# Giving each partition 128 KiB of neighbouring memory per turn, instead of two places 8 MiB apart

## The chip, the cores and the metric

The kernel runs on one core of a Trainium2 chip; the other cores are idle. The metric is the device time of that core in microseconds (us). Executions of one kernel agree within about 0.1%, unless said otherwise. A ratio is the mean time of one kernel's fast runs over that of the other's of the same rounds, so not quite the ratio of the medians quoted beside it.

## The reference

The backward pass of log-softmax over the last axis, in fp32:

```python
# y, dy: (8, 1024, 8192) fp32, so 8192 rows of 8192
softmax_x = np.exp(y)
sum_dy = np.sum(dy, axis=-1, keepdims=True)
return (dy - softmax_x * sum_dy).astype(np.float32)
```

Each element of y and dy is read once and each element of the result is written once: three tensors of 268.44 MB, 805.3 MB in all.

## The kernel before

The 8192 rows form 32 groups of 256; a partition holds two rows (64 KiB) of a group. A turn of the loop treats two groups. Three tiles of 64 KiB per partition exist: `x_ts[0]` and `x_ts[1]` for dy, overwritten by the result, and one `y_t`, which both groups of a turn share. The sums are split between VectorE (first row) and ScalarE (second row). Exp runs on ScalarE, multiply-add on VectorE, in pieces. All DMAs are issued by SyncE.

```python
y_v = y.flatten_outer_dims().rearrange("(g p r) d -> g p (r d)", p=P, r=R)      # R = 2
dy_v = dy.flatten_outer_dims().rearrange("(g p r) d -> g p (r d)", p=P, r=R)
out_v = out.flatten_outer_dims().rearrange("(g p r) d -> g p (r d)", p=P, r=R)
# ... (pools, tiles, sums() and compute() cut)
def load_dy(g, x):
    nc.sync.dma_start(out=x[:], in_=dy_v[g])
def load_y(g, lo, hi):
    nc.sync.dma_start(out=y_t[:, lo:hi], in_=y_v[g][:, lo:hi])
# ...
for g in range(0, G, 2):
    load_dy(g, x_ts[0])
    load_y(g, 0, W)
    s_t = sums(x_ts[0])
    for r in range(R):
        compute(x_ts[0], s_t, r)
    load_dy(g + 1, x_ts[1])
    s_t = sums(x_ts[1])
    for r in range(R):
        load_y(g + 1, r * D, (r + 1) * D)
        compute(x_ts[1], s_t, r)
    for j in range(2):
        nc.sync.dma_start(out=out_v[g + j], in_=x_ts[j][:])
```

## Time and profile before

| | before |
|---|---|
| time, median of the three runs known at the prediction | 1866.96 us (1866.71 to 1867.38) |
| span of the profiled run | 1865.9 us |
| VectorE / ScalarE busy | 46% / 37% |
| DMA queue: share of the 16 engines' time | 99.9% |
| rate over the span | 432 GB/s |

Read it from the bottom up. A queue that keeps 16 DMA engines busy for 99.9% of the span leaves nothing for anything else to bound, provided that the engines are not slow while busy.

### The profile page before, as it was taken

How to read it: one execution, taken by the hardware profiler on the slowest of the kernel's cores; microseconds unless marked ns; L12 is line 12 of the kernel's file. 1: busy time of each engine (PE TensorE's matmuls, PEld its weight loads, DVE VectorE, ACT ScalarE, POOL GpSimd, SP SyncE). 2: the span in 40 equal slices, each digit the busy share in tenths (PEclk: the TensorE clock that was granted, in tenths of full speed). 3: DMA queues.
4: the chain of work that ended last, by engine and by line, in shares of the span. 5: the costliest groups of instructions: out<-in, count | busy, mean ns of one | idle time of the engine just before them, and what ended most of it. 6: DMA issues, size and time to landing. Idle time of an engine off the chain costs nothing.

```text
span 1865.9 us, 923 instructions
## 1 busy us (share of the span) xinstructions
DVE 859.8 (46%) x256; ACT 698.7 (37%) x321; POOL 0.2 (0%) x4
## 2 busy tenths in 40 slices
DVE  2907429074290732807328073280632806338063
ACT  2606326063260532605336052360523605236052
POOL 0000000000000000000000000000000000000000
DMA  9999999999999999999999999999999999999999
GB/s 427 424 430 427 430 447 427 427 431 445 427 427 441 426 437 434 438 431 427 437 438 429 433 428 440 434 431 437 425 438 436 433 436 425 439 433 436 434 428 391
DMA packets 16135, 805.37 MB, mean 432 GB/s; under 512 B 1792, under 2 KB 1792, under 8 KB 1792
## 3 DMA queue, kind: packets, MB, share of 16 engines
q1 hardware_dynamic: 16128, 805.31, 99.9%
q14 instruction: 7, 0.06, 0.0%
HBM read 536.87 MB, written 268.44 MB: 432 GB/s over the span
## 4 chain that ended last, share of the span: by engine, by line
DMA 64%; DVE 13%; ACT 10%; another core or an unknown queue 9%; issue 1%; SPq 0%; DVEq 0%; ACTq 0%
DMA x<-in_dy_dram 31%; DMA out_dram<-x 30%; DVE x L81 13%; ACT copied L61 6%; ACT y_t L80 4%; DMA y_t<-in_y_dram 3%; SPq L75 0%; DVEq L128 0%; ACTq L128 0%; SPq L52 0%; ACTq L80 0%; ACTq L61 0%
## 5 line engine op out<-in xcount | busy, mean ns | idle before, releaser
L81 DVE SCALAR_TENSOR_TENSOR x<-y_t,s_t,x 128x3072 f32<-128x3072 f32 (+1 forms) x192 | 579.4, 3059 | 255.7 <-ACT y_t L80 255.7
L57 DVE TENSOR_REDUCE s_t<-x 128x1 f32<-128x8192 f32 x32 | 277.8, 8682 | 722.3 <-DMA x<-in_dy_dram 722.3
L80 ACT ACTIVATE y_t<-y_t 128x3072 f32<-128x3072 f32 (+1 forms) x192 | 460.1, 2466 | 269.4 <-DMA y_t<-in_y_dram 253.2
L61 ACT ACTIVATE copied<-x 128x4096 f32<-128x4096 f32 x64 | 229.6, 3587 | 864.9 <-DMA x<-in_dy_dram 863.9
L61 ACT ACTIVATION_READ_ACCUMULATOR copied<-x 128x1 f32 x64 | 11.9, 186 | 0.0
L64 DVE TENSOR_SCALAR s_t<-half_t 128x1 f32<-128x1 f32 x32 | 6.5, 204 | 0.0
L61 ACT ACT_TABLE_LOAD x1 | 1.3, 1283 | 0.7 <-PEq L117 0.7
L117 POOL MEMSET const-bfloat16-1.0<- 128x1 bf16 x1 | 0.1, 101 | 0.0
L117 POOL MEMSET const-uint8-127<- 128x1 uint8 x1 | 0.1, 101 | 0.0
L117 POOL MEMSET const-float32-0.0<- 128x1 f32 x1 | 0.1, 98 | 0.2 <-issue 0.2
L117 POOL MEMSET const-float32-1.0<- 128x1 f32 x1 | 0.1, 98 | 0.0
## 6 DMA issues: line engine op xcount, KB each, us to landing
y_t<-in_y_dram SPq DMA_DIRECT2D x32, 4096.0 KB, 18.1
x<-in_dy_dram SPq DMA_DIRECT2D x32, 48.3
out_dram<-x SPq DMA_DIRECT2D x32, 32.5
y_t<-in_y_dram SPq DMA_DIRECT2D x16, 57.6
```

Of the source, the lines that this page charges most:

```text
L57: nc.vector.tensor_reduce(out=s_t[:, 0:1], in_=x[:, :D], axis=mybir.AxisListType.X, op=ALU.add, negate=True)
L61: nc.scalar.activation(copied[:], x[:, D + h * H : D + (h + 1) * H], COPY, accum_out=half_t[:, h : h + 1])
L64: nc.vector.tensor_scalar(out=s_t[:, 1:2], in0=half_t[:, 0:1], scalar1=half_t[:, 1:2], scalar2=-1.0, op0=ALU.add, op1=ALU.mult,)
L80: nc.scalar.activation(y_t[:, cs], y_t[:, cs], EXP)
L81: nc.vector.scalar_tensor_tensor(out=x[:, cs], in0=y_t[:, cs], scalar=s_t[:, r : r + 1], in1=x[:, cs], op0=ALU.mult, op1=ALU.add,)
L117: nc = _bacc.Bacc("TRN2", target_bir_lowering=False, num_devices=1)
```

## The change

Its intent is better locality in memory: over a turn each partition reads and writes four neighbouring rows (128 KiB), the first half with the first group and the second with the second. Before, its two places in a turn were 8 MiB apart. Only the views change:

```diff
-    y_v = y.flatten_outer_dims().rearrange("(g p r) d -> g p (r d)", p=P, r=R)
+    y_v = y.flatten_outer_dims().rearrange("(t p j r) d -> t j p (r d)", p=P, j=2, r=R)
     # dy_v and out_v likewise
-        nc.sync.dma_start(out=x[:], in_=dy_v[g])
+        nc.sync.dma_start(out=x[:], in_=dy_v[g // 2, g % 2])
-        nc.sync.dma_start(out=y_t[:, lo:hi], in_=y_v[g][:, lo:hi])
+        nc.sync.dma_start(out=y_t[:, lo:hi], in_=y_v[g // 2, g % 2][:, lo:hi])
-            nc.sync.dma_start(out=out_v[g + j], in_=x_ts[j][:])
+            nc.sync.dma_start(out=out_v[g // 2, j], in_=x_ts[j][:])
```

Inside one DMA the distance between neighbouring partitions' runs of 64 KiB so goes from 64 KiB (one unbroken block of 8 MiB) to 128 KiB (every other 64 KiB of a block of 16 MiB).

More of the change, by code (lines that the diff above doesn't have):

```diff
@@ L38 @@
     PIECES = [(0, 2048), (2048, 5120), (5120, D)]
-    y_v = y.flatten_outer_dims().rearrange("(g p r) d -> g p (r d)", p=P, r=R)
-    dy_v = dy.flatten_outer_dims().rearrange("(g p r) d -> g p (r d)", p=P, r=R)
-    out_v = out.flatten_outer_dims().rearrange("(g p r) d -> g p (r d)", p=P, r=R)
+    y_v = y.flatten_outer_dims().rearrange("(t p j r) d -> t j p (r d)", p=P, j=2, r=R)
+    dy_v = dy.flatten_outer_dims().rearrange("(t p j r) d -> t j p (r d)", p=P, j=2, r=R)
+    out_v = out.flatten_outer_dims().rearrange("(t p j r) d -> t j p (r d)", p=P, j=2, r=R)
     pool = ctx.enter_context(tc.tile_pool(name="pool", bufs=1))
```

## The prediction

> **What bounds the kernel now.** One core computes dy − exp(y)·sum(dy) over 8192 rows of 8192 fp32. The rows go in 32 groups of 256, two rows (64 KiB) to a partition. I read first the page's head: the engines' busy times, the forty slices and the DMA queues.
>
> ```profile
> span 1865.9 us, 923 instructions
> ...
> DVE 859.8 (46%) x256; ACT 698.7 (37%) x321; POOL 0.2 (0%) x4
> ...
> DMA  9999999999999999999999999999999999999999
> GB/s 427 424 430 427 430 447 427 427 431 445 427 427 441 426 437 434 438 431 427 437 438 429 433 428 440 434 431 437 425 438 436 433 436 425 439 433 436 434 428 391
> DMA packets 16135, 805.37 MB, mean 432 GB/s; under 512 B 1792, under 2 KB 1792, under 8 KB 1792
> ...
> q1 hardware_dynamic: 16128, 805.31, 99.9%
> ...
> HBM read 536.87 MB, written 268.44 MB: 432 GB/s over the span
> ```
>
> The compute engines work for less than half of the span. The 16 DMA engines are at nine tenths or more in all forty slices, and the one queue's packets take 99.9% of the sixteen engines' time. No slice but the last (391) falls below 424 GB/s. The bytes are the least that the task allows: two inputs and one output of 268.44 MB each, 805.3 MB.
>
> A busy DMA engine can still be a slow one, so next I took the single packet records of the trace. There are 10,240 packets of 64 KiB, 4,096 of 32 KiB (the y loads of the second group, which come in halves) and 1,792 of 4 bytes (112 issues by 16 engines: the completion marks). A 64 KiB packet took 2418 ns at the least, 2418 at the median, 2422 at the 95th percentile and 2420 in the mean. A 32 KiB packet took 1213 at the 5th percentile, 1214 at the median and 1226 in the mean. 65,536 B / 2418 ns is 27.1 GB/s, times 16 is 433.7 GB/s. Loads and stores, alone or mixed, all sit on that one value. This looks like a fixed rate of the engine, not like a memory that answers now sooner, now later.
>
> Then the chain of waits that ended last, one turn of it (two groups):
>
> ```profile
> 333.81 38.67 DMA x<-in_dy_dram
> 372.56 3.72 ACT copied L61 x2
> 376.30 3.71 ACT copied L61 x2
> 380.01 11.82 another core or an unknown queue
> 391.91 4.57 ACT y_t L80 x2
> 399.84 12.34 DVE x L81 x4
> 412.57 37.35 DMA out_dram<-x
> 449.94 38.63 DMA x<-in_dy_dram
> ```
>
> A turn starts every 449.94 − 333.81 = 116.13 us. It moves 2 groups × 3 tensors × 8 MiB = 50.33 MB, and 50.33 MB / 433.7 GB/s = 116.05 us. So the turn is as long as its transfers at the rate of the engines. (Over 14 turns, from 101.02 to 1729.72 in the same view, the mean is 116.3 us.) The compute pieces in the chain look like 28 us without DMA, but they aren't. The stretches of the same turn show it (columns: stretch, its length, busy time of DVE, ACT and POOL, clock, DMA share, GB/s):
>
> ```profile
> 333.00:372.00 39.00, 0.00 (x0) 0.00 (x0) 0.00 (x0) 1.00 1.01 437
> 372.00:412.00 40.00, 26.66 (x8) 22.47 (x11) 0.00 (x0) 1.00 0.97 421
> 412.00:450.00 38.00, 27.09 (x9) 21.11 (x10) 0.00 (x0) 1.00 1.03 442
> ```
>
> While the engines compute (second stretch) the DMA share is still 0.97: transfers issued earlier drain in those moments. (A share over 1 comes from packets counted where they start.) The waits agree: the compute engines wait for loads, and the issuing sequencer waits for buffers while there is work in the DMA queue.
>
> ```profile
> ACT copied L61 <- DMA x<-in_dy_dram: 863.9, 32, 51.1
> DVE s_t L57 <- DMA x<-in_dy_dram: 722.3, 16, 46.9
> ```
>
> **What the Trainium skill says.** (1) "DMA: Bandwidth & Descriptors", section "Where 436 GB/s comes from", gives 435.2 GB/s as the ceiling of the 16 ports to SBUF. The trace agrees: 433.7 GB/s within packets, 432 over the span. (2) "HBM Reference", section "Specifications (TRN2)", gives some 716 GB/s for a memory domain and says that a core streaming alone is bounded by its 16 DMA engines. The uniform 2418 ns agrees; that leaves memory unused, by an estimate from that page's figure, 716 − 432 = 284 GB/s if the partner core is idle. (3) The DMA page, section "The descriptor swizzle", puts four neighbouring partitions on one engine and the next four on the next. The trace as read here doesn't show which engine takes which address, so no run shows it. (4) The DMA page, section "Latency and other measured facts", has the row about row pitch in HBM: copies of 128 × 16 KiB tiles ran at 207 GB/s per direction with 512 KiB between the partitions' rows, 164 with 2 MiB and 103 with 4 MiB, against 214 with padding. It says that aliasing of memory channels is only inferred. The kernel before has 64 KiB between partitions and nothing to see of this, at 2418 ns for nearly every packet.
>
> **The change part by part.** It alters only the three views of memory. Partition p in a turn took row pairs p and 128 + p of a 16 MiB block of each tensor: two places 8 MiB apart. Now it takes four neighbouring rows, 128 KiB, the first half with the first group, the second with the second.
>
> - Instructions: comparing the built kernels engine by engine, the same rows come in the same order with the same waits; only line numbers move by one. There are 112 DMA issues before and after. Cost: 0.
> - Descriptors: a partition's share of an issue is still a single run of 64 KiB (32 KiB for the split y loads). So 10,240 + 4,096 + 1,792 packets remain. At the durations before, (10,240 × 2420 + 4,096 × 1226 + 1,792 × 9 ns) / 16 = 1548.8 + 313.9 + 1.0 = 1863.7 us per engine. That is the whole span but 2 us. Cost: 0.
> - Nothing merges into 128 KiB transfers: the halves go to different buffers at different times.
> - Addresses: the distance between neighbouring partitions within one issue goes from 64 to 128 KiB; between streams of neighbouring engines, by (3), from 256 to 512 KiB. This is the only physical change. It matters only if a packet's duration then leaves 2418 ns. By (4), the first step of loss listed, 214/207 = 1.034, comes at 512 KiB per partition, four times what the new kernel has, and the loss grows with the pitch. I take 0 to 0.3% at 128 KiB, with 0.0% likeliest.
> - Compute: the same sizes, below half of the span, hidden beside transfers. Cost: 0.
>
> The sum is 1867.0 + 0 = 1867 us.
>
> **The rivals.** *Better locality makes it faster.* The intent suggests it. But time can come only out of what packets take above their least. With 2418 and 1213 ns as the floor, the excess over all packets, divided by 16 engines, is 1.3 us for the 64 KiB ones (among them 14 of the very first packets, at 2.6 to 3.3 us) and 3.3 us for the 32 KiB ones. If all of it went, 1867.0 − 4.6 = 1862.4 us, 0.25% less. Over 2% would need packets shorter than any of the 10,240 seen.
>
> *The doubled pitch makes memory channels collide.* For it: powers of two all through, and a row in the skill that shows such a loss. Against it: the pitch is below the least listed there, and runs are 64 KiB, not 16. Taken at the full 3.4% of 512 KiB the time would be 1930 us; at a quarter of it (an estimate, linear in the pitch) 1867 × 1.0085 = 1883 us.
>
> *Only the mixed stretch suffers.* About a third of a turn has loads and stores in flight together (the 412 to 450 stretch begins with it), and here 32 KiB packets of 1.3 to 1.6 us show up already. If each of the 4,096 took 10% more, 4,096 × 121 ns / 16 = 31 us would be added if nothing hid it: 1898 us, 1.7%. Nothing in the addresses says why this should come, so it is remote.
>
> **Range and chances.** The centre is the sum, 1867 us. Runs before spread over 0.7 us. Down, at most 4.6 us of excess can go, and I allow half of it: 1864. Up, 0.3% of small collisions: 1873. So 1864 to 1873 holds it 8 times in 10. Faster by over 2% (below 1829.6 us) would break the packets' floor: 0.005. Slower by over 2% (above 1904.3) needs channel collisions of over half of those at a four times greater pitch: 0.04. The rest, 0.955, is the same.
>
> **What will show it.** Right: the 64 KiB packet's median at 2418 ns, the queue's share at 99.9%, 432 GB/s over the span, turns of 116.3 us in the mean, and the waits of DVE and ACT for dy at 722 and 864 us within a few us. Wrong by collisions: packets of 2500 ns and more in many turns, GB/s below 424 in most slices at an unchanged busy share. Wrong by locality: fewer packets above the floor at the start and in the halves of y, and a span some us shorter. Wrong in the mechanism altogether: a DMA share below nine tenths somewhere, which would mean that the order of issues or waits had changed after all.

## The result, and the profile after

| | before | after |
|---|---|---|
| time, median of four runs | 1867.17 us (1866.71 to 1867.60) | 1866.88 us (1866.58 to 1867.27) |
| span of the profiled run | 1865.9 us | 1865.3 us |
| 64 KiB packets, median / mean | 2418 / 2420 ns | 2418 / 2420 ns |
| 64 KiB packets over 1.04 times the median | 32 of 10,240 | 18 of 10,240 |
| 32 KiB packets, median / mean | 1214 / 1226 ns | 1216 / 1221 ns |

The ratio is 0.9999, with a 95% interval of 0.9981 to 1.0016: the same. The page of the changed kernel (slices, packets, queue) answers line by line to that of before:

```profile
span 1865.3 us, 923 instructions
...
DMA  9999999999999999999999999999999999999998
GB/s 427 426 429 427 438 439 427 429 435 441 427 433 443 424 432 444 431 429 429 444 430 430 443 421 438 436 438 429 428 446 429 429 437 428 438 434 440 430 427 387
DMA packets 16135, 805.37 MB, mean 432 GB/s; under 512 B 1792, under 2 KB 1792, under 8 KB 1792
...
q1 hardware_dynamic: 16128, 805.31, 99.8%
```

The packet counts are equal to the last one, so nothing merged and nothing was split; the slices' rates stay in the same band, and the queue's share is 99.8% against 99.9%. The chain of one turn in the changed kernel (start, length, what), the turn shown before:

```profile
333.66 38.61 DMA x<-in_dy_dram
...
372.35 3.72 ACT copied L62 x2
...
412.38 37.34 DMA out_dram<-x
...
449.73 38.63 DMA x<-in_dy_dram
```

The turn is 449.73 − 333.66 = 116.07 us long, against 116.13 in the same place before. The waits for dy did not move either (us in total, times, longest); they were 863.9 and 722.3 us:

```profile
ACT copied L62 <- DMA x<-in_dy_dram: 863.7, 32, 51.0
DVE s_t L58 <- DMA x<-in_dy_dram: 721.1, 16, 46.8
```

### The profile page after: what moved, and what is told of

It is laid out like the page before. It is cut to its first block, busy times and chain, and to the rows that moved or that the text cites. A ratio compares the mean times of both kernels' runs of the same rounds, so it can differ in the third digit from the quotient of the medians.

```text
span 1865.3 us, 923 instructions
## 1 busy us (share of the span) xinstructions
DVE 859.9 (46%) x256; ACT 698.7 (37%) x321; POOL 0.2 (0%) x4
## 3 DMA queue, kind: packets, MB, share of 16 engines
q1 hardware_dynamic: 16128, 805.31, 99.8%
## 4 chain that ended last, share of the span: by engine, by line
DMA 64%; DVE 13%; ACT 10%; another core or an unknown queue 10%; issue 1%; SPq 0%; DVEq 0%; ACTq 0%
DMA x<-in_dy_dram 31%; DMA out_dram<-x 30%; DVE x L82 13%; ACT copied L62 6%; ACT y_t L81 4%; DMA y_t<-in_y_dram 3%; SPq L76 0%; DVEq L129 0%; ACTq L129 0%; SPq L53 0%; ACTq L81 0%; ACTq L62 0%
```

## The experiments

A null result can mean that the disputed thing costs nothing, that it is hidden, or that two effects cancel. The theory: each DMA engine moves 64 KiB in 2418 ns whatever the addresses, as long as memory answers in time, and at 128 KiB between partitions it does. The rivals: collisions that begin near by, a cancellation between loads and stores, a cost in the chain of waits that busy DMA engines mask, and a bound that is memory's rather than the engines'. Twelve kernels ran. Where single packets are told of, they were taken from the trace's packet records, which the views don't print.

**e1, 512 KiB, and e2, 2 MiB between partitions.** The same edit with larger blocks; the results stay right.

```diff
-    y_v = ... rearrange("(t p j r) d -> t j p (r d)", p=P, j=2, r=R)    # the changed kernel
+    y_v = ... rearrange("(t p j r) d -> t j p (r d)", p=P, j=8, r=R)    # e1; j=32 in e2
```

> Layout with 512 KiB between neighbouring partitions in each issue (eight groups share a block) instead of 64 KiB before and 128 KiB after; result stays right. Theory (the DMA engines' own rate of 2418 ns per 64 KiB packet sets the time, memory has room): 1867 us, within 0.3%, median packet 2418 ns. Rival (distance between partitions makes memory channels collide, the change was just below the onset): 3.4% slower as the Trainium skill's row for 512 KiB says, some 1930 us, packets of 2500 ns.

> The largest distance these tensors allow: 2 MiB between neighbouring partitions, each partition owning 64 neighbouring rows over the whole kernel; result stays right. Theory: 1867 us, packets still at 2418 ns[...]. Rival (collisions, by the skill's 164 against 214 GB/s at 2 MiB): a factor of 1.30, some 2430 us, packets near 3150 ns. In between, 1900 to 2300: collisions exist but long runs soften them.

e1: 1892.87 us (1882.48 to 1900.96), ratio 1.0132 (1.0095 to 1.0169). e2: 1967.32 us (1958.96 to 1977.31), ratio 1.0536 (1.0505 to 1.0567); before in the same rounds 1867.69. The theory's number fell in both, and the rival's size fell too: the loss exists, but it is 1.3% and 5.4%, not 3.4% and 30%. The time of e2 lies in the in-between range of its expectation, but no run tests the reason given there, that long runs soften the loss. Head and queue of e2:

```profile
span 1957.2 us, 923 instructions
...
DMA  9999999999999999999999999999999999999999
GB/s 368 418 364 427 432 390 434 400 427 434 406 431 399 426 413 413 429 387 428 405 410 427 387 428 405 413 426 391 429 402 421 421 396 425 413 414 429 394 425 376
...
q1 hardware_dynamic: 16128, 805.31, 99.8%
...
HBM read 536.87 MB, written 268.44 MB: 411 GB/s over the span
```

This is what a real address effect looks like: the busy share is the same 99.8%, and the rate has dips to 364 to 400. A busy share cannot tell a fast engine from a slow one. Its chain says where the dips are: the load of dy that starts while the last store is still under way took 42.3 us instead of 38.7.

```profile
318.07 37.65 DMA out_dram<-x
...
355.74 42.32 DMA x<-in_dy_dram
...
475.98 42.39 DMA x<-in_dy_dram
```

**e6, 256 KiB between partitions** (j=4).

> 256 KiB between neighbouring partitions, between the changed kernel's 128 KiB (ratio 0.9999) and 512 KiB (1.0132). Theory (loss grows with the distance from an onset above 128 KiB): ratio 1.000 to 1.008. Rival (512 KiB was slow for another reason, such as eight groups sharing a block): exactly 1.000 within 0.2%, or over 1.013.

1867.97 us, ratio 1.0002 (0.9985 to 1.0018), 35 slow packets of 10,240, as before. It came out in the corner that I had given to the rival ("exactly 1.000"), so it cannot rule out that eight groups to a block matter for another reason. It does say that the changed kernel is a factor of two or more away from any loss. Sorted by start, the 64 KiB packets of a turn come in five blocks of 128, one to a DMA (at the edges two DMAs mix). Mean ns:

| kernel | distance | ratio | dy, 1st | y | dy, 2nd | store, 1st | store, 2nd | packets over 1.04 × median |
|---|---|---|---|---|---|---|---|---|
| before | 64 KiB | 1 | 2425 | 2419 | 2420 | 2419 | 2418 | 32 |
| after | 128 KiB | 0.9999 | 2423 | 2419 | 2422 | 2419 | 2418 | 18 |
| e6 | 256 KiB | 1.0002 | 2424 | 2419 | 2421 | 2419 | 2419 | 35 |
| e1 | 512 KiB | 1.0132 | 2474 | 2418 | 2419 | 2419 | 2452 | 310 |
| e2 | 2 MiB | 1.0536 | 2628 | 2437 | 2430 | 2468 | 2778 | 2169 |
| e7, loads only | 2 MiB | 1.0160 | 2522 | 2438 | 2422 | 2418 | 2429 | 672 |
| e8, stores only | 2 MiB | 1.0369 | 2522 | 2418 | 2419 | 2512 | 2759 | 1671 |

**e3, the changed layout for the loads alone** (stores as before; rows land in the wrong place).

```diff
-    out_v = ... "(t p j r) d -> t j p (r d)"    # the changed kernel
+    out_v = ... "(g p r) d -> g p (r d)"
```

> Only the loads of y and dy have the changed layout, the stores the old one; rows land in the wrong place on purpose. Theory (both parts cost nothing): ratio 1.000 within 0.2%. Rival (the change helps one side and hurts the other, and they cancel): ratio off by 0.5% or more, to either side.

1867.56 us, ratio 1.0000 (0.9986 to 1.0013). So there is no gain in the loads that a loss in the stores would cancel.

**e4, all transfers, no computation.** The calls of `sums` and `compute` are left out of the kernel before.

```diff
-        s_t = sums(x_ts[0])
-        for r in range(R):
-            compute(x_ts[0], s_t, r)
     # the same for x_ts[1]; all loads and stores stay
```

> Layout of before, all 112 issues, but no computation at all (wrong result on purpose: the output is dy). Theory (transfers at the engines' rate are the whole time, computation is covered): 1862 to 1867 us, not over 0.4% faster. Rival (the waits of the chain through sums, exp and multiply-add, 28 us a turn, cost something that the DMA share hides): 1840 us or less, down to 1600 if all of them counted.

1866.72 us, ratio 0.9995 (0.9981 to 1.0008). Its output is dy itself; it was still reported as correct, since the subtracted term is too small for the comparison's tolerance here, which is worth knowing when "correct" is read. The stretches of the turn, with the columns of the prediction but without DVE and ACT, which have nothing to show:

```profile
333.00:372.00 39.00, 0.00 (x0) 1.00 1.00 432
372.00:412.00 40.00, 0.00 (x0) 1.00 0.97 420
412.00:450.00 38.00, 0.00 (x0) 1.00 1.02 441
```

They are those of before to within 5 GB/s. The 28 us of sums, exp and multiply-add that the chain shows in every turn cost nothing together, measurably. So a layout that feeds the compute engines earlier has nothing to gain either.

**e7 and e8: 2 MiB on one side only** (wrong rows).

> Only the loads have 2 MiB between partitions, the stores the 64 KiB of before; wrong rows on purpose. With both sides the ratio was 1.0536, and the slow packets were the first of a turn's load of dy (2.7 to 3.3 us) and the last of the store before it (3.6 to 3.8), where the two are in flight together. Theory A (loads and stores collide with each other only if both have the large distance): ratio below 1.015. Theory B (each side's own distance slows it): about half of it, 1.02 to 1.035, with slow loads and stores at 2418 ns.

> Only the stores have 2 MiB between partitions, the loads 64 KiB; wrong rows on purpose. Theory A: below 1.015. Theory B: 1.02 to 1.035, with slow stores and loads at 2418 ns. Both sides slow in only one of these two runs would say that one direction alone brings it about.

e7: 1897.04 us, ratio 1.0160 (1.0145 to 1.0176). e8: 1937.74 us, ratio 1.0369 (1.0347 to 1.0390). The two losses, 1.6% and 3.7%, add up to the 5.4% of e2 within the intervals. Theory A, that it takes a large distance on both sides, has fallen: each side alone has a loss clear of noise. (Its limit of 1.015 is passed clearly by e8, and only just by e7, whose interval begins at 1.0145.) Theory B is right about there being a loss from each side, but not in its sizes, nor in who suffers: with large stores the first load of dy, whose own layout is that of before, is at 2522 ns too (table; with the packets followed engine by engine as far as they could be, so that stores are left out, 2524). Theory A's remaining part, that loads and stores must be in flight together, was put to the test by itself.

**e9 and e10: loads kept apart from stores**, e9 with 2 MiB, e10 as a control with 64 KiB. The two x tiles change roles each turn, so that the first load waits for the last store, and two one-column copies make the other loads wait for the first. (Only the last half load of y still meets the first store, for 2.4 to 4.2 us a turn in e9.)

```diff
     for g in range(0, G, 2):
+        xs = x_ts if g % 4 == 0 else x_ts[::-1]     # xs in place of x_ts below
         load_dy(g, xs[0])
+        nc.vector.tensor_copy(out=y_t[:, :1], in_=xs[0][:, :1])
+        nc.vector.tensor_copy(out=xs[1][:, :1], in_=xs[0][:, :1])
```

> 2 MiB between partitions on both sides, but no load of the next turn is issued before both stores have landed (the buffers change roles each turn, and two one-column copies make the other loads wait for the first); right result. Some bubbles of about 2 us, two or three a turn, are added: 60 to 120 us. Theory (the slow packets need loads and stores in flight together): means of 64 KiB packets fall from 2548 ns to below 2440 and the ratio to its control e10_apart64k is below 1.015. Rival (the distance alone slows packets, mixed or not): mean stays near 2550, ratio to the control 1.04 to 1.06.

> The control for e9_apart2m: the same order of transfers with the 64 KiB of before. Expected 60 to 120 us slower than before by the added bubbles, 64 KiB packets at 2418 ns in the median and 2420 in the mean.

e9: 2148.09 us, ratio to before 1.1510. e10: 1968.64 us, ratio 1.0540. Of e10's added 101 us, by the packet records, some 66 are idle time of the engines and 35 are longer packets. Between the two 1.1510 / 1.0540 = 1.092; of this difference (170 us between the profiled runs) 123 us are longer packets and the rest is more idle time. The 64 KiB packets of e9 took 2662 ns in the mean, more than in e2, where nothing was kept apart; those of e10 took 2452, where I had expected 2420. My theory said that they would fall below 2440: it has fallen. Even the rival's 1.04 to 1.06 was too small. Split by steps of 16 packets, the first step of a turn's first load of dy took 3461 ns in e9 and 3091 in e10, and the later ones 2555 to 2738 in e9 and 2418 to 2420 in e10. So two things are shown. At 2 MiB loads alone are slow, without a store beside them; and after a pause the first packets are slow at both distances. What is not shown is why the loads of y in e2, which start with no pause, stay near 2437 ns. One guess is that pauses put the engines back in step, while in a steady stream they drift apart. The kept traces speak against it as the whole cause. Let 1 mean that the sixteen engines start their packets at one moment, and 0 that the starts are evenly spread: e9 has 0.59 and 0.55 in the first two loads after pauses, but 0.29 in the second load of dy, as spread as in e2 (0.28). Yet that load's packets took 2624 ns in e9 and 2430 in e2. The cause stays open.

**e5, e11 and e12: what the 2418 ns belong to.** Three measurements by themselves; results are wrong, and each ran once. The loop of the kernel before is taken out; e5 loads `x_ts[0]` first, and in all three 32 ordinary stores follow.

```diff
+    for n in range(24):                                             # e5
+        nc.sync.dma_start(out=x_ts[1][:], in_=x_ts[0][:])
+        nc.sync.dma_start(out=y_t[:], in_=x_ts[0][:])
+    for g in range(G):                                              # e11
+        for k in range(0, P, 8):
+            nc.sync.dma_start(out=x_ts[g % 2][k : k + 8], in_=dy_v[g][k : k + 8])
+    for g in range(G):                                              # e12
+        for k in range(16):
+            k0 = 32 * (k % 4) + k // 4
+            nc.sync.dma_start(out=x_ts[g % 2][k0 : k0 + 29 : 4], in_=dy_v[g][k0 : k0 + 29 : 4])
```

> A measurement by itself (wrong result on purpose): after one load, 48 copies of a whole 8 MiB tile from SBUF to SBUF, 64 KiB per partition, with no access to device memory in that stretch; then 32 stores with nothing beside them. Theory (a packet's 2418 ns is the rate of the DMA engine and its path to SBUF): a 64 KiB packet takes 2418 ns in the copies too, or somewhat more if read and write share the path, and 2418 in the stores. Rival (2418 ns is what device memory gives): copies clearly faster, 2300 ns or less.

In the copies the median packet took 3782 ns, in the stores after them 2422. That rules the rival out in its form: without device memory packets are slower, not faster. But it doesn't show the theory right, because to read and write SBUF at once is another job than a load from memory.

> A measurement by itself (wrong result on purpose): dy is loaded in pieces of eight partitions, which I expect to run on eight of the 16 DMA engines only, then 32 ordinary stores. Theory (2418 ns is each engine's own rate): 64 KiB packets of the loads still at 2418 ns, DMA share 0.5, about 217 GB/s in that stretch. Rival (2418 ns is a share of a common limit of memory or fabric): packets well below 2418, down to 1209 ns.

The loads ran at 62 GB/s, with a median packet of 8264 ns. The run missed its question. What slowed it isn't shown: beside e12, both the partitions and the places in memory of the eight packets lie closer together (64 KiB apart in memory against 256), and no run separates the two. e12 repairs that:

> e11 put eight packets at a time into eight neighbouring partitions and measured 62 GB/s, so [...]it did not answer its question. The same measurement with the eight partitions four apart (0, 4, ... 28 and so on), again on eight of 16 DMA engines; wrong result on purpose. Theory (2418 ns is the rate of one DMA engine and its path): loads' packets at 2418 ns, DMA share 0.5, some 217 GB/s while loading. Rival (2418 ns is a sixteenth of a common limit in memory or fabric): packets well below 2418 ns, as only eight share it. If packets are again far above 2418, the SBUF side is not told apart and the question stays open.

The stretches of e12, during loads and during stores (length, POOL's busy time, clock, DMA share, GB/s):

```profile
100.00:1100.00 1000.00, 0.00 (x0) 1.00 0.50 217
1350.00:1800.00 450.00, 0.00 (x0) 1.00 1.00 433
```

Through 1230 us of loads exactly eight packets were in flight. With half of the engines at work so, the loads' packets took 2418 ns at the median and 2421 in the mean. The DMA share was 0.50 and the rate 217 GB/s, exactly as the theory had it. If memory or a common fabric had set the pace for sixteen engines, eight of them would have been quicker. So the 2418 ns of a load belong to the engine and its own way. Stores were not tried with fewer engines.

No version faster than the two kernels came out of this. e4 has all the bytes and no work at all, and is within 0.2% of them.

## Why the prediction was right

- **What bounds the kernel.** The prediction took a fixed rate of the DMA engines from the uniform 2418 ns. e12 shows it for the loads (half the engines, the same packet), and e4 shows that nothing but the transfers makes up the time.
- **Instructions, descriptors, merging: cost 0.** The page after has the same 923 instructions and the same packets. Right.
- **Addresses: 0 to 0.3%, 0.0 likeliest.** Measured −0.01%, with packets at 2418 ns. e3 shows that this isn't a cancellation, and e6 that twice the distance is free as well. Here the prediction had some luck. That 128 KiB costs nothing was a judgement: its 0.3% was not worked out, its own proportional estimate gave 0.85%, and nothing that it had seen showed where the loss begins. A fixed rate of the engines alone doesn't promise it, as e1 shows at 512 KiB.
- **Compute: cost 0.** Right: VectorE was busy for 859.9 us against 859.8, and without any compute the time is the same (e4).
- **Rival "better locality".** At most 4.6 us were to be had. The excess of the 32 KiB packets went from 3.3 to 2.1 us per engine, and the time moved by 0.3 us, within the spread of the runs. No gain is shown.
- **Rival "collisions".** A loss by distance exists, as e1 and e2 show, but the prediction oversized it and gave it the wrong shape; that memory channels collide is not shown. It took 3.4% at 512 KiB from the skill's row; this kernel lost 1.3%. It scaled that in proportion to the distance, to 0.85% at 128 KiB; measured is nothing up to 256 KiB, then a rise. Even the 2 MiB of e2 lost only 5.4%, where the row would give 30%. The row's tiles have 16 KiB per partition and it is about copies between two places in memory; these runs differ in both, and none here separates the two.
- **Rival "only the mixed stretch suffers".** Not at 128 KiB. The prediction also misread the size of that stretch. Loads and stores are issued and not yet landed together for a third of a turn, but the packets come almost in order of issue: in the kernel before, packets of y and of the next store ran at once for 0.5 us of the first turn, up to 3.9 in the later ones. At 512 KiB and 2 MiB the slow packets of a continuous stream sit mostly where a store ends and a load begins, but e9 shows that loads alone can be slow too.

## What to carry to other kernels

When every DMA engine is busy all the time and nearly every packet takes one and the same time, as here, ask whether that time is the engine's own, as e12 does. Here it was: a new layout with the same packets had at most 4.6 us to win, while larger distances lost up to 5.4%. The durations of packets show such a loss where a busy share doesn't. Keep the runs of neighbouring partitions close: for runs of 64 KiB, distances up to 256 KiB were free here, 512 KiB cost 1.3% and 2 MiB 5.4%. A version without the compute takes a minute to write and says whether anything beside the transfers can matter.

## What the Trainium skill lacked or had wrong

- "DMA: Bandwidth & Descriptors", section "Latency and other measured facts", row on row pitch in HBM: it lists copies of 16 KiB rows only (207, 164 and 103 GB/s against 214). For loads and stores of 64 KiB runs the loss is much smaller: none at 64, 128 and 256 KiB, 1.3% at 512 KiB, 5.4% at 2 MiB. At 2 MiB it is also unequal: 1.6% with the loads' layout alone changed, 3.7% with the stores'.
- The same row doesn't say that the order of transfers matters: at 2 MiB the 64 KiB packets averaged 2548 ns in a continuous stream (e2) and 2662 with pauses between stores and loads (e9). Why is not shown.
- The same page has latencies for the start of a transfer, but doesn't say, as far as I found, how much longer the first packets after a pause are in a trace: the first sixteen 64 KiB packets of the kernel before had a median of 3.09 us, and in e10 the first step of a load after each pause 3.09 in the mean, against 2.42.
- The same page, section "Where 436 GB/s comes from", says that for SBUF to SBUF the fabric's 435 GB/s bind. e5's copies within the partitions ran at 273 GB/s, with packets of 3782 ns (one run).
- That section also says that between HBM and SBUF some 358 GB/s bind. With one core active, the kernels here ran at 432 GB/s, and e12 shows the engines as the bound. For a core alone the page that the prediction cites under (2) has it right.
